# Differential attention in a hybrid decoder block: the causal mask added by TensorE, and the two softmax maps combined with one scaling

## The chip, the cores and the metric

The kernel runs on one core of a Trainium2 chip. The metric is the device time of one execution in microseconds (us), the median over several runs. The engines are named as in the profile: PE is TensorE's matmul stream and PEld its weight loads, DVE is VectorE, ACT is ScalarE, POOL is GpSimd, and SP is SyncE, which here only issues DMA transfers.

## What is computed

One decoder layer for 512 tokens of width 1024: an input projection feeds two groups of heads side by side (differential attention and an RWKV-7 mixer), then come an output projection, an expert layer (PEER) that takes most of the time, a gated per-layer embedding and a last norm. The change lies in the differential attention, which has 4 heads, two score maps for each head, and an RMS norm over the 128 output columns of each head:

```python
def diff_attention(z_da, positions, lam_q1, lam_k1, lam_q2, lam_k2, subln_g, lam_init):
    ...
    lam = (jnp.exp(jnp.sum(lam_q1.astype(f32) * lam_k1.astype(f32)))
           - jnp.exp(jnp.sum(lam_q2.astype(f32) * lam_k2.astype(f32))) + lam_init)
    key_pos = jnp.arange(S)

    def block(bi):
        start = bi * Q_BLOCK
        qb = lax.dynamic_slice_in_dim(q, start, Q_BLOCK, axis=3)
        s = jnp.einsum('bhcqd,bhckd->bhcqk', qb, k).astype(f32)
        causal = key_pos[None, :] <= (start + jnp.arange(Q_BLOCK))[:, None]
        pr = jax.nn.softmax(jnp.where(causal, s, -jnp.inf), axis=-1)
        a = pr[:, :, 0] - lam * pr[:, :, 1]
        return jnp.einsum('bhqk,bhkv->bhqv', a.astype(v.dtype), v)
    ...
    o = rms_norm(o, subln_g) * (1.0 - lam_init)
```

## The kernel before

Tokens are worked on in four blocks of 128 (b = 0 to 3). The attention of one block is `da_block`. For each head h it runs both maps c = 0, 1: a matmul on 64 rows of the array (map 0 on rows 0 to 63, map 1 on rows 64 to 127) writes the scores of the block's queries against the nk = 128 (b + 1) keys seen so far into a PSUM tile `psS` (L753); DVE adds the mask to the last 128 columns of it (L754); DVE takes the row maximum (L756); ACT writes the exponentials to `pexp` and their row sum to `st` (L757). With both maps done, DVE inverts the two sums (L758), multiplies one by minus lambda (L759), scales map 0 (L760) and adds the scaled map 1 (L761). PE turns the result around (`pta`, L765), ACT copies it out (`ah`, L769), and after the fourth head PE multiplies with the values (`po`, L776), ACT squares, and DVE does the norm (L780, the small steps of `rstd`, L783). A float32 matmul is two instructions in the trace, so the 32 score matmuls are 64 rows.

`da_block` is a generator that yields after each head, and `mixers` weaves it with three others: `rw_solve` (a chain of small DVE steps, L582 and L584, that solves triangular systems), `rw` (the RWKV states, all engines) and `ple_proj` (matmuls into `accr`, copied by ACT into `pp` and stored by DMA to `pd`, L800). A scheduler then orders the instructions of every engine by its own estimate of when each is ready; each engine, and SP's queue of DMA issues, works strictly in that order. So an instruction that is taken away or added also moves others.

Three things around the change are spoken of below. First, the tiles `pexp`, `ah`, `sol_u` and `xg` share one ring of 14 buffers, so a `pexp` may have to wait until another tile is read for the last time. Second, for each block `rw_solved` loads `xg`, `tt`, `bhr`, `ykr`, `bk` and `uv` through SP's queue (L601 to L613); PE then makes `pwu` (L620), ACT `wu` (L621), PE `pmt` (L632, which reads `bhr`) and `prp` (L639). Third, the constants are made by POOL in `mixer_consts`, between the squares of the input (L838, L840, L842), whose sum gives the row scales of the first norm (`pss`, L847).

Of the kernel before, what the change touches and what calls it, by code (L numbers as in the profile page):

```python
# [24 lines left out]
NEG = -3.0e38  # L25
EPS = 1e-6
# [27 lines left out]
class Kernel:  # L54
# [188 lines left out]
    def mixer_consts(self, pool):  # L243
        nc, a = self.nc, self.a

        def same_chunk(t, keep_le=None):
# [12 lines left out]
            elif keep_le == 2:  # L259
# [19 lines left out]
        self.causal = pool.tile([128, 128], F32, name="causal")  # L279
        nc.gpsimd.memset(self.causal, 0.0)  # L280
        nc.gpsimd.affine_select(self.causal, self.causal, pattern=[[-1, 128]], base=0, channel_multiplier=1,
                                compare_op=OP.is_ge, fill=NEG)

# [456 lines left out]
    def da_block(self, b, qT, kT, vs, psum, out):  # L740
# [4 lines left out]
        av = []  # L745
        for h in range(4):
            st = sm.tile([128, 4], F32, name="sm")
            pq = self.p4("pexp", [128, 2, 512])
            p = [pq[:, 0], pq[:, 1]]
            for c in range(2):  # L750
                o = slice(64 * c, 64 * c + 64)
                ps = psum.tile([128, 512], F32, name="psS", tag="acc", bufs=4)
                nc.tensor.matmul(ps[:, :nk], qT[o, h, :], kT[h // 2][o, h % 2, :nk], start=True, stop=True)  # L753
                nc.vector.tensor_tensor(ps[:, b * 128:nk], ps[:, b * 128:nk], self.causal, op=OP.add)  # L754
                mx = st[:, c:c + 1]
                nc.vector.tensor_reduce(mx, ps[:, :nk], axis=AX.X, op=OP.max, negate=True)  # L756
                nc.scalar.activation(p[c][:, :nk], ps[:, :nk], AF.Exp, bias=mx, accum_out=st[:, 2 + c:3 + c])  # L757
            nc.vector.reciprocal(st[:, 2:4], st[:, 2:4])  # L758
            nc.vector.tensor_mul(st[:, 3:4], st[:, 3:4], self.nlam)  # L759
            nc.vector.tensor_scalar(p[0][:, :nk], p[0][:, :nk], st[:, 2:3], None, op0=OP.mult)  # L760
            nc.vector.scalar_tensor_tensor(p[0][:, :nk], p[1][:, :nk], st[:, 3:4], p[0][:, :nk], op0=OP.mult,  # L761
                                           op1=OP.add)
# [10 lines left out]
        ss = sm.tile([128, 4], F32, name="oss")  # L773
        for h in range(4):
# [5 lines left out]
        nc.vector.tensor_reduce(ss, sq, axis=AX.X, op=OP.add)  # L780
        r = self.rstd(sm, ss, 128, EPS, cols=4, name="ors")
        for h in range(4):
            nc.vector.scalar_tensor_tensor(out[:, h * 128:h * 128 + 128], po[:, h, :], r[:, h:h + 1], self.subln,  # L783
                                           op0=OP.mult, op1=OP.mult)
# [817 lines left out]
```

## Time and profile before

| what | value |
|---|---|
| runs | 1864.88, 1874.73, 1876.71 us; median 1874.73 us |
| the profiled execution's own time | 1859.81 us |
| its span (first to last instruction) | 1857.4 us |
| mean granted TensorE clock in it | 0.966 of full speed |
| stretch in which `da_block` runs (start of its first psS matmul to start of its last L783) | 289.7 to 452.2 us |

The profile gives for each engine how long it was busy, for each group of instructions (line of the source, engine, operation, tiles) its count, its busy time and the mean of one, and what ended the idle time before it. The timeline has one row for each instruction, or for several like ones in a run: start, duration, engine, line, tiles, count, and in brackets how long the engine had been idle before and what released it. In the timeline the start of the next row on an engine says more than the duration, since matmuls, and DVE instructions that don't depend on each other, overlap at their ends. A view of stretches gives busy times and the granted clock between two points of time.

### The profile page before, as it was taken

How to read it: one execution, taken by the hardware profiler on the slowest of the kernel's cores; microseconds unless marked ns; L12 is line 12 of the kernel's file. 1: busy time of each engine (PE TensorE's matmuls, PEld its weight loads, DVE VectorE, ACT ScalarE, POOL GpSimd, SP SyncE). 2: the span in 40 equal slices, each digit the busy share in tenths (PEclk: the TensorE clock that was granted, in tenths of full speed). 3: DMA queues.
4: the chain of work that ended last, by engine and by line, in shares of the span. 5: the costliest groups of instructions: out<-in, count | busy, mean ns of one | idle time of the engine just before them, and what ended most of it. 6: DMA issues, size and time to landing. Idle time of an engine off the chain costs nothing.

```text
span 1857.4 us, 28657 instructions
## 1 busy us (share of the span) xinstructions
PE 1728.6 (93%) x10434; PEld 1465.3 (79%) x10434; DVE 1448.7 (78%) x3233; ACT 739.5 (40%) x1371; POOL 653.0 (35%) x447
## 2 busy tenths in 40 slices
PE   6887987897998987999999999999999999999998
PEld 5755665666777787998777788889899999989886
DVE  6476587667459999987888787887878787878786
ACT  3424342332335654444443433333333333333354
POOL 6662121110126664001111133334545555555530
PEclk9988997889999998999999999999999999999999
DMA  5533224441442343445665678777989898989891
GB/s 171 154 95 97 81 83 91 100 118 34 150 145 83 109 129 100 140 142 192 208 203 201 195 240 272 237 265 274 310 308 310 308 310 305 311 308 313 303 329 65
DMA packets 149842, 361.62 MB, mean 195 GB/s; under 512 B 43859, under 2 KB 58447, under 8 KB 149573
## 3 DMA queue, kind: packets, MB, share of 16 engines
q1 hardware_dynamic: 109924, 221.89, 37.2%
q0 software_dynamic: 36864, 134.23, 21.3%
q10 hardware_dynamic: 2912, 3.67, 0.7%
q8 instruction: 82, 1.34, 0.3%
q14 instruction: 60, 0.48, 0.1%
HBM read 330.51 MB, written 21.36 MB: 189 GB/s over the span
## 4 chain that ended last, share of the span: by engine, by line
PE 68%; DVE 22%; issue 4%; ACT 3%; DMA 1%; POOL 1%; ACTq 0%; SPq 0%; DVEq 0%; POOLq 0%
PE po L1270 21%; PE phid L1134 8%; PE phid L1136 8%; PE phid L1135 8%; PE pg L1239 2%; DVE wlo L132 2%; ACT whi L128 2%; PE acc L201 2%; DVE ids L1083 2%; PE acc L202 2%; PE acc L200 2%; DVE wlo L134 1%; PE psA L538 1%; DVE rest L977 1%; DVE jj L1227 1%
## 5 line engine op out<-in xcount | busy, mean ns | idle before, releaser
L132 DVE TENSOR_TENSOR wlo<-wraw,whi 128x1024 fp32r<-128x1024 f32 x243 | 297.6, 1225 | 150.5 <-ACT whi L128 150.4
L128 ACT ACTIVATE whi<-wraw 128x1024 fp32r<-128x1024 f32 x276 | 291.4, 1057 | 177.7 <-PE phid L1135 59.0
L1136 PE MATMUL phid<-u2dhi,wlo 128*128 128x384 f32 x1024 | 347.7, 340 | 12.7 <-POOL wlo L132 12.7
L1134 PE MATMUL phid<-u2dhi,whi 128*128 128x384 f32 x1024 | 350.9, 343 | 1.0 <-ACT row L1143 1.0
L1135 PE MATMUL phid<-u2dlo,whi 128*128 128x384 f32 x1024 | 346.9, 339 | 0.0
L1293 POOL DMA_INDIRECT row<-in_peer_u_dram,idx x128 | 190.7, 1490 | 404.5 <-DVE row L1305 222.2
L1293 POOL DMA_INDIRECT row<-in_peer_v_dram,idx x128 | 186.1, 1454 | 276.8 <-DVE h L1309 194.8
L1270 PE MATMUL po<-whi,chi 128*128 128x512 f32 x768 | 243.9, 399 | 1.2 <-ACT row L1143 1.2
L1270 PE MATMUL po<-whi,clo 128*128 128x512 f32 x768 | 243.1, 398 | 1.5
L1270 PE MATMUL po<-wlo,chi 128*128 128x512 f32 x768 | 241.4, 395 | 0.0
L1136 PEld LDWEIGHTS phid<-u2dhi,wlo 128*128 128x128 f32 x1024 | 194.7, 190 | 14.8 <-POOL wlo L132 14.8
L1134 PEld LDWEIGHTS phid<-u2dhi,whi 128*128 128x128 f32 x1024 | 194.8, 190 | 5.8 <-ACT row L1143 1.3
L1135 PEld LDWEIGHTS phid<-u2dlo,whi 128*128 128x128 f32 x1024 | 194.4, 190 | 3.7
L1270 PEld LDWEIGHTS po<-whi,clo 128*128 128x128 f32 x768 | 143.0, 188 | 42.0 <-DVE clo L134 8.7
L1270 PEld LDWEIGHTS po<-wlo,chi 128*128 128x128 f32 x768 | 144.4, 188 | 34.3
L1309 DVE SCALAR_TENSOR_TENSOR h<-row,ids,h 128x1024 f32<-128x1024 f32 x128 | 164.0, 1281 | 1.5
L128 ACT ACTIVATE chi<-gelu 128x384 fp32r<-128x384 f32 x128 | 67.4, 526 | 239.8 <-DVE gelu L1247 121.5
L1270 PEld LDWEIGHTS po<-whi,chi 128*128 128x128 f32 x768 | 141.1, 188 | 25.5 <-ACT row L1143 1.5
L1305 DVE SCALAR_TENSOR_TENSOR row<-row,xn 128x1024 f32<-128x1024 f32 x128 | 153.8, 1220 | 0.0
L1143 ACT ACTIVATE gelu<-phid 128x384 f32<-128x384 f32 x86 | 42.3, 492 | 266.9 <-PE phid L1136 266.9
L200 PE MATMUL acc<-whi,uhi 128*128 128x512 f32 (+1 forms) x224 | 91.1, 416 | 18.8 <-ACT whi L128 11.6
L132 POOL TENSOR_TENSOR wlo<-wraw,whi 128x1024 fp32r<-128x1024 f32 x33 | 78.8, 2400 | 68.9 <-ACT whi L128 68.9
(436 smaller groups left out, 2938.0 us busy)
## 6 DMA issues: line engine op xcount, KB each, us to landing
wraw<-in_peer_uT_dram SPq DMA_DIRECT2D x128, 512.0 KB, 3.9
wraw<-in_peer_v_dram SPq DMA_DIRECT2D x128, 512.0 KB, 6.2
wraw<-in_w_in_dram SPq DMA_DIRECT2D x24, 512.0 KB, 6.1
wraw<-in_peer_w_q_dram SPq DMA_DIRECT2D x16, 512.0 KB, 4.4
ahead<-row SPq DMA_DIRECT2D x42, 192.0 KB, 2.3
gelu<-ahead SPq DMA_DIRECT2D x42, 192.0 KB, 3.8
wraw<-in_w_out_dram SPq DMA_DIRECT2D x8, 512.0 KB
zp<-z ACTq DMA_DIRECT2D x12, 224.0 KB, 2.7
```

Of the source, the lines that this page charges most:

```text
L128: self.last_hi = nc.scalar.activation(hi, src, AF.Copy, **({} if g is None else {"scale": g}))
L132: self.last_lo = eng.tensor_tensor(lo, src, hi.bitcast(F32), op=OP.subtract)
L200: nc.tensor.matmul(o, hi[:, k, s], whi, start=(k == 0), stop=False)
L201: nc.tensor.matmul(o, hi[:, k, s], wlo, start=False, stop=False)
L1134: nc.tensor.matmul(ps, whi[:, s], hi[:, k, :], start=(k == 0), stop=False)
L1135: nc.tensor.matmul(ps, whi[:, s], lo[:, k, :], start=False, stop=False)
L1136: nc.tensor.matmul(ps, wlo[:, s], hi[:, k, :], start=False, stop=(k == KC - 1))
L1143: nc.scalar.activation(g, ps, AF.Gelu)
L1270: nc.tensor.matmul(outs[b, e], lhs[:, s], rhs[:, 512 * e:512 * e + 512], start=(c == 0 and rhs is vhi and lhs is chi), stop=(c == NKEY - 1 ...
L1293: nc.gpsimd.indirect_dma_start(out=row, out_offset=None, in_=a["peer_u" if kind == "U" else "peer_v"], in_offset=bass.IndirectOffsetOnAxis ...
L1305: nc.vector.scalar_tensor_tensor(row, row, 1.0, xn0, op0=OP.mult, op1=OP.mult, accum_out=hid0[:, k:k + 1])
L1309: nc.vector.scalar_tensor_tensor(acc0, row, hid0[:, k:k + 1], acc0, op0=OP.mult, op1=OP.add)
```

## The change

The mask becomes a matmul: after each score matmul PE multiplies an identity with the 128x128 mask and accumulates it onto the last 128 columns of `psS`. Mask and identity are copied by POOL into tiles of the matmul type fp32r, and the masked value is -2^127. DVE no longer adds the mask.

Map 0 is left unscaled. With the sums s0 and s1 of the exponentials, DVE forms f = (s0 / s1) times minus lambda and adds f times map 1 to map 0; the result is s0 times what it was. That factor is taken out at the end: the reciprocals r0 of the four s0 (one instruction for each block) multiply the sum of squares twice ahead of the norm's square root and the norm's factor once behind it. The statistics of a block lie in one tile `st` of 128x4x4 and not in one for each head.

```diff
+MASK = -2.0 ** 127
...
-        self.causal = pool.tile([128, 128], F32, name="causal")
-        nc.gpsimd.memset(self.causal, 0.0)
-        nc.gpsimd.affine_select(self.causal, self.causal, pattern=[[-1, 128]], base=0, channel_multiplier=1,
-                                compare_op=OP.is_ge, fill=NEG)
+        causal = pool.tile([128, 128], F32, name="causal")
+        nc.gpsimd.memset(causal, 0.0)
+        nc.gpsimd.affine_select(causal, causal, pattern=[[-1, 128]], base=0, channel_multiplier=1,
+                                compare_op=OP.is_ge, fill=MASK)
+        self.causal = pool.tile([128, 128], F32R, name="causal_r")
+        nc.gpsimd.tensor_copy(self.causal, causal)
+        self.ident_r = pool.tile([128, 128], F32R, name="ident_r")
+        nc.gpsimd.tensor_copy(self.ident_r, self.ident)
...
+        st = sm.tile([128, 4, 4], F32, name="sm")
         for h in range(4):
-            st = sm.tile([128, 4], F32, name="sm")
...
-                nc.vector.tensor_tensor(ps[:, b * 128:nk], ps[:, b * 128:nk], self.causal, op=OP.add)
-                mx = st[:, c:c + 1]
+                nc.tensor.matmul(ps[:, b * 128:nk], self.ident_r, self.causal, start=False, stop=True,
+                                 skip_group_check=True)
+                mx = st[:, c, h:h + 1]
                 nc.vector.tensor_reduce(mx, ps[:, :nk], axis=AX.X, op=OP.max, negate=True)
-                nc.scalar.activation(p[c][:, :nk], ps[:, :nk], AF.Exp, bias=mx, accum_out=st[:, 2 + c:3 + c])
-            nc.vector.reciprocal(st[:, 2:4], st[:, 2:4])
-            nc.vector.tensor_mul(st[:, 3:4], st[:, 3:4], self.nlam)
-            nc.vector.tensor_scalar(p[0][:, :nk], p[0][:, :nk], st[:, 2:3], None, op0=OP.mult)
-            nc.vector.scalar_tensor_tensor(p[0][:, :nk], p[1][:, :nk], st[:, 3:4], p[0][:, :nk], op0=OP.mult,
-                                           op1=OP.add)
+                nc.scalar.activation(p[c][:, :nk], ps[:, :nk], AF.Exp, bias=mx, accum_out=st[:, 2 + c, h:h + 1])
+
+            f = sm.tile([128, 1], F32, name="smf")
+            nc.vector.reciprocal(f, st[:, 3, h:h + 1])
+            nc.vector.scalar_tensor_tensor(f, f, st[:, 2, h:h + 1], self.nlam, op0=OP.mult, op1=OP.mult)
+            nc.vector.scalar_tensor_tensor(p[0][:, :nk], p[1][:, :nk], f, p[0][:, :nk], op0=OP.mult, op1=OP.add)
...
+        r0 = sm.tile([128, 4], F32, name="osr")
+        nc.vector.reciprocal(r0, st[:, 2, :])
...
+        for _ in range(2):
+            nc.vector.tensor_mul(ss, ss, r0)
         r = self.rstd(sm, ss, 128, EPS, cols=4, name="ors")
+        nc.vector.tensor_mul(r, r, r0)
```

In the changed source the lines stand a little lower: the score matmul is L760 there, the mask matmul L761. The scheduler's order shows at three places what moved. A row is one instruction, or several like ones in a run (x2): its line, its operation, the tile it writes and those it reads, and the shape. Ring numbers behind a name are of no matter here.

PE, block 1, heads 0 and 1. `psS` are the scores, `accr` the matmuls of `ple_proj`, `py` those of the RWKV output. Before:

```order
L753 MATMUL psS<-kT_1064,qT 128x256 x2
L236 MATMUL accr<-whi,phi 128x512
L237 MATMUL accr<-wlo,phi 128x512
L238 MATMUL accr<-whi,plo 128x512
L236 MATMUL accr<-whi,phi 128x512
L237 MATMUL accr<-wlo,phi 128x512
L238 MATMUL accr<-whi,plo 128x512
L699 MATMUL py<-state,rtT 32x64 x12
L753 MATMUL psS<-kT_1064,qT 128x256 x2
L236 MATMUL accr<-whi,phi 128x512
L237 MATMUL accr<-wlo,phi 128x512
L238 MATMUL accr<-whi,plo 128x512
```

Now, from the second head on:

```order
L705 MATMUL py<-state,rtT 32x64 x12
L760 MATMUL psS<-kT_1068,qT 128x256
L761 MATMUL psS<-causal_r,ident_r 128x128
L760 MATMUL psS<-kT_1068,qT 128x256
L773 MATMUL pta<-ident,pexp 128x128 x2
L697 MATMUL py<-wu,arb 128x64 x4
L705 MATMUL py<-state,rtT 32x64 x12
L761 MATMUL psS<-causal_r,ident_r 128x128
L237 MATMUL accr<-whi,phi 128x512
L238 MATMUL accr<-wlo,phi 128x512
L239 MATMUL accr<-whi,plo 128x512
```

The two scores of a head stood next to each other; now a mask matmul on all rows of the array stands between them, and the second mask, with the `accr` behind it, comes after two groups of `py`.

SP's queue, the loads for block 1 of the RWKV part. `tt`, `bhr` and `ykr` are loads, `pd` is the store of a `pp` that ACT has yet to write. Before:

```order
L603 DMA xg<-d_xg_82 128x1024
L601 DMA tt<-td_79 32x8x32 x4
L800 DMA pd_70<-pp 128x512
L605 DMA bhr<-d_bh_86 128x1x512
L606 DMA ykr<-d_yk_98 128x512
L613 DMA bk<-d_bh_86 32x16x64
```

Now:

```order
L609 DMA xg<-d_xg_82 128x1024
L607 DMA tt<-td_79 32x8x32 x4
L611 DMA bhr<-d_bh_86 128x1x512
L813 DMA pd_70<-pp 128x512
L612 DMA ykr<-d_yk_98 128x512
L619 DMA bk<-d_bh_86 32x16x64
```

The load of `bhr`, which waits for no engine but only for its place in the queue, now stands ahead of the store. The other loads keep their places behind it.

POOL, near the start of the program. `xt` are the squares of the input and their sums, the rest are constants. Before:

```order
L280 MEMSET causal 128x128
L275 AFFINE_SELECT chunk_ind<-chunk_ind 128x4
L281 AFFINE_SELECT causal<-causal 128x128
L838 TENSOR_TENSOR xt<-xt 128x1024
L277 AFFINE_SELECT chunk_ind<-chunk_ind 128x4
L840 TENSOR_TENSOR xt<-xt 128x1024
```

Now:

```order
L282 MEMSET causal 128x128
L276 AFFINE_SELECT chunk_ind<-chunk_ind 128x4
L288 CAST ident_r<-ident 128x128
L278 AFFINE_SELECT chunk_ind<-chunk_ind 128x4
L283 AFFINE_SELECT causal<-causal 128x128
L851 TENSOR_TENSOR xt<-xt 128x1024
L286 CAST causal_r<-causal 128x128
L853 TENSOR_TENSOR xt<-xt 128x1024
```

The two copies stand in the middle of the squares, ahead of six more of them.

## The prediction

> **What bounds the kernel now.** First the page's head: the whole span, and how busy the engines are in it.
>
> ```profile
> span 1857.4 us, 28657 instructions
> PE 1728.6 (93%) x10434; PEld 1465.3 (79%) x10434; DVE 1448.7 (78%) x3233; ACT 739.5 (40%) x1371; POOL 653.0 (35%) x447
> ```
>
> PE is the busy engine of the whole, but that is an average over stages; the change lies in the attention stage of about 165 us. So I read next the stretches of that stage (us from:to, length; then for PE, PEld, DVE, ACT and POOL the busy time and in brackets the instructions; then the granted clock, the DMA share and GB/s).
>
> ```profile
> 289.40:324.10 34.70, 21.59 (x139) 15.47 (x137) 29.32 (x83) 7.47 (x22) 5.33 (x4) 0.67 0.38 72
> 324.10:349.00 24.90, 23.10 (x225) 16.80 (x225) 15.93 (x65) 9.17 (x29) 0.96 (x1) 0.84 0.36 101
> 349.00:363.80 14.80, 10.32 (x107) 8.45 (x107) 7.93 (x29) 5.28 (x17) 0.00 (x0) 0.77 0.69 134
> 363.80:390.00 26.20, 23.88 (x271) 16.61 (x270) 21.43 (x70) 9.15 (x22) 8.22 (x6) 1.00 0.49 132
> 390.00:408.00 18.00, 17.47 (x121) 11.65 (x120) 10.58 (x29) 6.12 (x16) 3.27 (x3) 0.62 0.30 75
> 408.00:447.00 39.00, 36.18 (x508) 28.34 (x508) 24.71 (x83) 11.01 (x26) 0.00 (x0) 0.96 0.16 32
> ```
>
> Three different limits stand here. Up to 324 us DVE is full (29.32 of 34.70) and PE waits. From 324 on PE is busy nearly all the time (97% at 390 to 408, 93% at 408 to 447), except at 349 to 363.8, where neither PE nor DVE is (10.32 and 7.93 of 14.80) and something else is late. And the clock is low in four of the six: at 0.62 a matmul takes half again as long. So work taken from DVE is worth something only before 324 and where PE waits for DVE, and work given to PE costs time nearly everywhere behind it. How much DVE work waits for PE and not the other way round, the group of the mask addition tells (count; busy us, mean ns; idle us before it and what ended it):
>
> ```profile
> L754 DVE TENSOR_TENSOR psS<-psS,causal 128x128 f32<-128x128 f32 x32 | 9.3, 295 | 23.7 <-PE psS L753 23.6
> ```
>
> These 32 additions are 9.3 us of DVE, but DVE had stood idle 23.6 us for the scores just ahead of twelve of them. Of what DVE saves there, much only lengthens a wait for PE.
>
> **The change, term by term.** The sum is made against the profiled execution's own time, 1859.81 us (its span of 1857.4 and 2.4 around it). That lies 14.92 below the median of the runs shown, 1874.73; the difference is scatter between executions, and I carry the sum over to the median.
>
> *Two copies on POOL, +0.7.* POOL makes constants and squares without a pause up to the last square, and PE waits for that one:
>
> ```profile
> 16.31 0.29 POOL L281 TENSOR_SCALAR_AFFINE_SELECT causal<-causal 128x128 f32<-128x128 f32 x1
> 16.58 1.89 POOL L838 TENSOR_TENSOR xt<-xt 128x1024 f32<-128x1024 f32 x1
> ...
> 33.78 0.38 PE L847 MATMUL pss<-ones,xt 128*128 128x1 f32 x2 [1.98 <-POOL xt L842]
> ```
>
> PE had been idle 1.98 us for the last sum, so whatever POOL gets in addition, PE gets too, and later stages with it. A select over the same 128x128 takes 0.27 from start to start (16.31 to 16.58), which makes 0.54 for two; POOL slows where DVE reads beside it, so I take 0.7, between 0.5 and 1.6. It cannot be a gain.
>
> *Solve stretch, 289 to 324: -1.0.* The chain here is the solve on DVE; at its end ACT, then PE start at once:
>
> ```profile
> 299.65 0.29 DVE L754 TENSOR_TENSOR psS<-psS,causal 128x128 f32<-128x128 f32 x1
> 299.85 0.32 DVE L582 TENSOR_TENSOR sol_p<-sol_x,sol_u 128x98 f32<-128x98 f32 x1
> ...
> 323.65 0.37 ACT L757 ACTIVATE pexp<-psS,sm 128x128 f32<-128x128 f32 x1 [11.60 <-issue]
> 324.16 0.58 PE L753 MATMUL psS<-kT,qT 64*128 64x128 f32 x1 [6.61 <-ACT pexp L757]
> ```
>
> ACT stood 11.60 us ahead of the exponential of head 2: by the order of the tiles its `pexp` takes the ring place of `sol_u`, whose last reader is the solve's last product, and PE's next scores wait 6.61 us for ACT. An addition among the solve steps costs 0.20 (299.65 to 299.85). Three additions and two scalings go from there, 5 x 0.20 = 1.0 (0.6 to 1.4). The masks of heads 0 to 2 that PE gets are hidden in its waits; if DVE were no longer the limit they would cost what the next term says.
>
> *Masks on PE from 324 on, +4.9.* Of the 32, 26 stand there: two of block 0, 24 of blocks 1 to 3. No row shows an fp32r matmul of 128 columns, so I bound it by matmuls of 128 columns that are there:
>
> ```profile
> 325.63 0.47 PE L765 MATMUL pta<-ident,pexp 128*128 128x128 f32 x1
> 326.04 0.47 PE L656 MATMUL pst<-uv,bk 64*64 64x64 f32 x3
> ...
> 370.76 0.44 PE L765 MATMUL pta<-ident,pexp 128*128 128x128 f32 x2
> 371.13 0.56 PE L656 MATMUL pst<-uv,bk 64*64 64x64 f32 x12
> ...
> 427.71 1.16 PE L776 MATMUL po<-dav,ah 128*128 128x128 f32 x8 [0.74 <-ACT ah L769]
> 428.70 1.95 PE L620 MATMUL pwu<-xg,tt 128*128 128x128 f32 x16
> 434.96 2.08 PE L677 MATMUL plg<-g_up,lg 128*128 128x512 f32 x2
> ```
>
> Among others of its own form, one costs (428.70 - 427.71) / 8 = 0.12. Between matmuls on fewer rows, a single one at the low clock costs 0.41 (325.63 to 326.04); a pair at full clock costs 0.37, so a single one about 0.37 - 0.12 = 0.25. In the order about half of the masks have a full-row matmul behind them, the rest stand between scores or states on 64 or 32 rows. I take 0.19, between 0.12 and 0.25: 26 x 0.19 = 4.9, with ends 3.1 and 10.7. It can't be below nothing, since an instruction is added to a full engine. [...]
>
> *Scores that no longer run side by side, +1.5.* Where both score matmuls of a head stand together, the second is free:
>
> ```profile
> 336.06 0.70 PE L753 MATMUL psS<-kT,qT 64*128 64x256 f32 x4
> 336.69 0.50 PE L236 MATMUL accr<-whi,phi 128*128 128x512 f32 x1
> ...
> 348.40 0.70 PE L753 MATMUL psS<-kT,qT 64*128 64x256 f32 x2 [0.26 <-ACT pp L799]
> ```
>
> Four instructions (both maps) take 0.70, and two (one map) take 0.70 as well; each map has its own half of the array. With a mask between them, which uses all rows and must follow the first, that is gone. From 324 on three heads had it in full: heads 0 and 1 of block 1, and head 0 of block 2. [...]
>
> *Loads of RWKV block 1, -5.3.* Here lies the gap of the third stretch. SP's queue, one row of ACT, and PE:
>
> ```profile
> 340.36 1.88 SPq L601 DMA_DIRECT2D tt<-td  x4
> 348.37 0.34 SPq L800 DMA_DIRECT2D pd<-pp  x1
> 348.75 0.59 SPq L605 DMA_DIRECT2D bhr<-d_bh  x1
> ...
> 351.11 0.60 ACT L621 ACTIVATE wu<-pwu 128x512 f32<-128x512 f32 x1 [0.30 <-PE pwu L620]
> ...
> 349.02 2.05 PE L620 MATMUL pwu<-xg,tt 128*128 128x128 f32 x16
> 355.46 0.45 PE L632 MATMUL pmt<-bhr,wu 32*64 32x64 f32 x8 [4.39 <-DMA bhr<-d_bh]
> 355.84 0.94 PE L753 MATMUL psS<-kT,qT 64*128 64x256 f32 x2
> 356.71 2.84 PE L632 MATMUL pmt<-bhr,wu 32*64 32x64 f32 x56
> 361.45 0.69 PE L765 MATMUL pta<-ident,pexp 128*128 128x128 f32 x2
> ```
>
> SP had issued `tt` at 342.24 and then stood until 348.37 at the store of `pp`, since ACT had not written it; `bhr`, which nothing held, stood behind it and came to PE only at 355.46, 4.39 us too late, though `wu` was there at 351.71. In the new order `bhr` is ahead of the store. So the wait ends with `wu`. The same work in block 3, where no load is late, takes 434.96 - 428.70 = 6.3 from `pwu` to the end of `prp`; block 1 takes 361.45 - 349.02 = 12.4, with one score matmul of 0.87 (355.84 to 356.71) in it. 12.4 - 0.87 - 6.3 = 5.3: 3.7 of it wait, the rest the low clock behind the idle time (0.77 in that stretch). Late next is `wu`, then `uv`, whose loads are still behind the store. Bounds: 2.0 if one of these takes the place of `bhr`, 6 with the low clock of the next matmuls. [...]
>
> *Where PE waits for DVE, -2.0.* There are three such places, the ends of the RWKV output of blocks 0, 1 and 2. The rows of the first:
>
> ```profile
> 345.90 0.30 DVE L754 TENSOR_TENSOR psS<-psS,causal 128x128 f32<-128x128 f32 x1
> 346.11 0.16 DVE L704 TENSOR_SCALAR mean<-mean 128x8 f32<-128x8 f32 x1
> 346.17 0.15 DVE L759 TENSOR_TENSOR sm<-sm,nlam 128x1 f32<-128x1 f32 x1
> 346.24 0.35 DVE L760 TENSOR_SCALAR pexp<-pexp,sm 128x256 f32<-128x256 f32 x1
> 346.51 0.69 DVE L705 TENSOR_TENSOR y<-y,mean 128x512 f32<-128x512 f32 x1
> ```
>
> An addition costs 0.21 (345.90 to 346.11), a scaling 0.27 (346.24 to 346.51), a small product 0.06 (346.11 to 346.17). Out go one addition and one scaling at 345.9, three and one at 381 to 388, two and one at 423 to 427: 6 x 0.21 + 3 x 0.27 = 2.1, less 0.1 for the new products. Bounds 1.0 and 3.0, the scaling being dearer with more columns.
>
> *Tail, +0.3.* The last block's three small products and a reciprocal stand in the DVE work that ends the stage: 0.06 to 0.2 each, so 0.2 to 0.6. The reciprocal and multiplication of each head replace their like, at nothing: same count, same size.
>
> Sum: 0.7 - 1.0 + 4.9 + 1.5 - 5.3 - 2.0 + 0.3 = -0.9 us. The profiled execution would take 1858.9, the median 1873.8. No difference that can be measured: about 1% (18.7 us) is what a measurement here can tell from none. Two large terms, the masks and the moved load, cancel; without the load, which the change was not about, it would be slower by 4.4.
>
> **The rivals.**
>
> *Every mask pays the dear price (slower than before).* Place: PE from 324 to 447. [...] For it speaks the 0.41 row; against it that this row was taken at half clock, and that half of the masks have a full-row neighbour. 26 x 0.41 = 10.7 in place of 4.9: +4.9, 1879.6. It decides from 0.23 each (0.19 + 0.9 / 26); to be slower by over 1% a mask would need 0.19 + 19.6 / 26 = 0.94, over twice the dearest row.
>
> *A half-clock stretch goes as well.* At 390 to 408 the granted clock was 0.62, so about 0.76 of 18 us were at half; PE was full, and at full clock the stretch would be shorter by up to 6.8. The stretch before it has short PE gaps that DVE made, which the change shortens, and masks fill some. I price it at 5: -5.9, 1868.8. Against it: no gap there was long, the work that fell idle is of the same kind as now, and a new slow stretch could as well appear elsewhere.
>
> *The load is hidden anyway.* If `uv` or ACT's copies set when the states can start, the 5.3 shrink to 2.0: +2.4, 1877.1. For it: `uv` keeps its place behind the store; against: PE reached a reader of `uv` only at 371.13, behind the second transposes, some 9 us after 361.45.
>
> *The relief of DVE is worth nothing.* If the three places wait for PE in turn, 2.0 and 1.0 go: +2.1, 1876.8. For it speak the 23.6 us of the mask's group, against it the rows at 345.9, where DVE has no idle time.
>
> **How the numbers follow.** Forecast 0.45, dear masks 0.20, clock 0.15, hidden load 0.10, no relief 0.10. The cases lie between 1868.8 and 1879.6. The runs of before reach from 9.9 below their median to 2.0 above it, so the range takes in that much more below (1868.8 - 9.9 = 1858.9) and above (1881.6; with no relief of DVE beside dear masks, +2.1, 1883.7): 1858 to 1884. Faster by over 1% (below 1856.0) needs the clock rival and a low set of runs, 0.06, a part of the clock's 0.15; slower by over 1% (above 1893.5) needs a mask price that no row shows, 0.04, a part of the dear masks' 0.20; within 1%, 0.90.
>
> **What would show it.** The wait of `pmt` for `bhr` is gone from the waits and PE's clock stays at 1.0 behind it (load). The scores stand as runs of two, never four, and a mask's start-to-start cost is 0.12 to 0.25 (masks). The solve's last product ends about 0.3 earlier in spite of 0.7 from POOL. DVE's busy time falls by the 9.3 of the additions and by the 16 scalings, less the new products, and its wait for scores moves to the maximum. The forecast is wrong if a mask takes 0.4 or more, if the idle time before `pmt` is still there under another name, or if the stage's length differs by more than 5 us.

## The result, and the profile after

| | before | after |
|---|---|---|
| median of the first comparison (8 runs each) | 1872.12 us | 1857.53 us |
| their range | 1863.18 to 1876.71 | 1854.85 to 1863.40 |
| ratio, 95% interval | | 0.9938, 0.9909 to 0.9966 |
| the profiled execution, its mean clock | 1859.81 us, 0.966 | 1863.40 us, 0.962 |

The changed kernel is faster by 0.6%, some 11 us, where 0.9 us was forecast: no difference by the bound of 1%, but clear of the measurement's own interval. The ratio puts the time at 1863.1 on the forecast's base (0.9938 x 1874.73), within the range; the raw median lies 0.5 under its lower end. And the profiled executions stand the wrong way round: the one of before was faster than any of its eight runs in the table, the one after the slowest of its eight. Two profiles alone would have said "slower by 3.6". What must be explained is a difference between two sets of executions, not between two traces.

The head of the page after:

```profile
span 1861.7 us, 28696 instructions
PE 1742.9 (94%) x10466; PEld 1475.0 (79%) x10466; DVE 1442.2 (77%) x3201; ACT 739.9 (40%) x1371; POOL 650.5 (35%) x449
```

The attention stage, cut at the same places of the program in both kernels: from PE's first `pwu` of a block to that of the next, and from the last one to PE's start behind its long wait for `olo`. Columns as before (stretch, length; PE, PEld, DVE, ACT, POOL; clock, DMA share, GB/s). Before:

```profile
296.18:349.02 52.84, 40.67 (x349) 30.20 (x348) 42.06 (x131) 14.05 (x45) 3.84 (x3) 0.72 0.31 70
349.02:390.44 41.42, 34.62 (x380) 25.50 (x380) 29.79 (x100) 14.41 (x38) 8.22 (x6) 0.92 0.55 131
390.44:428.70 38.26, 36.11 (x366) 25.50 (x366) 25.39 (x81) 11.71 (x29) 3.27 (x3) 0.82 0.26 60
428.70:461.42 32.72, 23.88 (x319) 19.27 (x317) 22.68 (x67) 11.04 (x21) 2.34 (x1) 0.90 0.09 18
```

After:

```profile
300.21:357.08 56.87, 47.82 (x361) 35.11 (x361) 41.81 (x121) 14.26 (x45) 3.83 (x3) 0.68 0.30 72
357.08:392.88 35.80, 34.56 (x391) 25.05 (x391) 26.62 (x77) 14.35 (x38) 7.96 (x6) 1.00 0.55 143
392.88:434.42 41.54, 39.62 (x374) 27.34 (x373) 24.66 (x82) 11.70 (x29) 3.22 (x3) 0.75 0.23 55
434.42:464.88 30.46, 21.91 (x319) 18.15 (x317) 22.27 (x67) 11.16 (x21) 2.34 (x1) 0.96 0.09 19
```

Together they take 165.24 and 164.67 us, so the two traces differ by 0.6 in the stage; the 3.6 us that the later one is longer came in before the stage, in code that was not changed, where its clock was lower (0.67 against 1.00 between 155 and 165 us). Within the stage the gains and losses are large: +4.0, -5.6, +3.3, -2.3. The last column but two, the clock, goes with those of blocks 1 and 2: it is 1.00 where it was 0.92, and 0.75 where it was 0.82.

The load's place. PE's rows and two of SP's queue in the trace after:

```profile
350.23 0.59 SPq L611 DMA_DIRECT2D bhr<-d_bh  x1
356.05 0.34 SPq L813 DMA_DIRECT2D pd<-pp  x1
...
357.08 2.00 PE L626 MATMUL pwu<-xg,tt 128*128 128x128 f32 x16
359.01 0.45 PE L638 MATMUL pmt<-bhr,wu 32*64 32x64 f32 x8
...
362.40 1.09 PE L645 MATMUL prp<-arb,wu 128*64 128x128 f32 x16 [0.48 <-ACT mt L640]
363.68 0.44 PE L773 MATMUL pta<-ident,pexp 128*128 128x128 f32 x2 [0.18 <-DVE pexp L770]
```

`bhr` is issued at 350.23, ahead of the store at 356.05, and `pmt` starts without a wait. From `pwu` to the end of `prp` block 1 takes 363.68 - 357.08 = 6.6 us in place of 12.4.

A mask's price, from one start to the next, on PE after:

```profile
343.08 0.70 PE L760 MATMUL psS<-kT,qT 64*128 64x256 f32 x2
343.70 0.33 PE L761 MATMUL psS<-causal_r,ident_r 128*128 128x128 f32 x1
343.96 0.70 PE L760 MATMUL psS<-kT,qT 64*128 64x256 f32 x2
344.58 0.33 PE L761 MATMUL psS<-causal_r,ident_r 128*128 128x128 f32 x1
344.75 0.45 PE L237 MATMUL accr<-whi,phi 128*128 128x512 f32 x1
```

Two score matmuls of a map 0.62, the mask 0.26 ahead of the next scores (343.70 to 343.96) and 0.17 ahead of a full-row matmul (344.58 to 344.75); so a head takes 1.67 where it took 0.63.

The solve, on DVE after:

```profile
319.24 0.29 DVE L764 TENSOR_REDUCE sm<-psS 128x1 f32<-128x128 f32 x1 [1.08 <-PE psS L761]
...
320.37 0.29 DVE L764 TENSOR_REDUCE sm<-psS 128x1 f32<-128x128 f32 x1 [0.58 <-PE psS L761]
```

The additions are gone, but the maximum waits in the chain of the solve for the mask, which stands behind `accr` on PE.

### The profile page after: what moved, and what is told of

It reads as the page before. It is cut to its first block, busy times and chain, and to the rows that moved or that the text cites. A ratio compares the mean times of both kernels' runs of the same rounds, so it can differ in the third digit from the quotient of the medians.

```text
span 1861.7 us, 28696 instructions
## 1 busy us (share of the span) xinstructions
PE 1742.9 (94%) x10466; PEld 1475.0 (79%) x10466; DVE 1442.2 (77%) x3201; ACT 739.9 (40%) x1371; POOL 650.5 (35%) x449
## 4 chain that ended last, share of the span: by engine, by line
PE 68%; DVE 23%; issue 4%; ACT 3%; DMA 1%; POOL 1%; ACTq 0%; SPq 0%; DVEq 0%; POOLq 0%
PE po L1283 21%; PE phid L1147 8%; PE phid L1149 8%; PE phid L1148 8%; PE pg L1252 2%; DVE wlo L133 2%; ACT whi L129 2%; DVE ids L1096 2%; PE acc L202 2%; PE acc L203 1%; PE acc L201 1%; PE psA L544 1%; PE psS L760 1%; DVE rest L990 1%; DVE wlo L135 1%
## 5 line engine op out<-in xcount | busy, mean ns | idle before, releaser
L202 PE MATMUL acc<-wlo,uhi 128*128 128x512 f32 (+1 forms) x224 | 92.9, 415 | 11.3 <-DVE wlo L135 11.2
```

The costliest lines, as they stand in the source:

```text
L202: nc.tensor.matmul(o, hi[:, k, s], wlo, start=False, stop=False)
```

## The experiments

Each ran against the kernel before on the same chip. The clock column is the mean over a kernel's runs of the granted clock; n counts its runs.

| kernel | edit | median us (n) | ratio, 95% interval | clock |
|---|---|---|---|---|
| b_again | before, unaltered | 1869.25 (12) | 0.9981, 0.9957 to 1.0004 | 0.9593 |
| a_again | after, unaltered | 1858.31 (7) | 0.9926, 0.9901 to 0.9951 | 0.9651 |
| mask_only | masks on PE, old scaling | 1860.37 (9) | 0.9946, 0.9921 to 0.9971 | 0.9653 |
| scale_only | unscaled map 0, masks on DVE | 1860.66 (10) | 0.9945, 0.9914 to 0.9976 | 0.9629 |
| b_pd | before, stores of `pp` on ACT's queue | 1872.89 (12) | 1.0021, 0.9998 to 1.0045 | 0.9560 |
| b_fill | before, with 32 matmuls of zeros | 1875.76 (12) | 1.0027, 1.0006 to 1.0048 | 0.9583 |
| s_pd | scale_only, stores on ACT's queue | 1852.65 (6) | 0.9915, 0.9886 to 0.9944 | 0.9650 |
| a_mask2 | after, each mask twice | 1864.76 (9) | 0.9968, 0.9953 to 0.9982 | 0.9650 |
| a_late1 | after, the stage ends 0.73 later | 1858.26 (12) | 0.9953, 0.9927 to 0.9979 | 0.9653 |
| a_late4 | after, the stage ends 2.9 later | 1863.14 (12) | 0.9982, 0.9956 to 1.0008 | 0.9622 |
| a_keep | after, zeros added between `pmt` | 1873.27 (12) | 1.0030, 1.0005 to 1.0054 | 0.9597 |
| a_add | after, 32 additions of zeros on DVE | 1868.60 (12) | 0.9985, 0.9960 to 1.0010 | 0.9626 |

### Both kernels again

> The changed kernel once more, unaltered, for a second profiled execution and for the ratio. The first profiled executions (1859.8 us before, 1863.4 after) are each at the edge of its kernel's runs, and the one after enters the attention stage 4.0 us later for reasons that lie in code that was not changed. Theory A (work: the path got shorter by the terms of the sum): the ratio stays near 0.994, and the profiled execution, near 1857, shows the attention stage (first scores to the wait for the last split) 5 to 11 us shorter than before. Theory B (clock: some executions of before lose a half-clock stretch that the changed kernel does not lose): the executions of before fall again in a group near 1864 and one near 1875, those of the changed kernel do not, and two executions of the same clock differ by no more than 3 us.

> The kernel before, unaltered, timed against itself: a ratio of 1.000 within 0.003. Theory A: a profiled execution of 1870 to 1876 us is longer than that of 1859.8 by waits in the attention stage or in front of it. Theory B: it has the same waits, but a mean granted clock of about 0.955 to 0.96 in place of 0.966, and the rows show one more stretch of some 10 to 20 us at half clock that the execution of 1859.8 did not have.

Every run lists its mean clock, and with that the two kernels come together. Over 109 runs of before (those that the experiments were compared with, and b_again) the clock lies between 0.951 and 0.968 and the time falls by 1.5 us for each 0.001 of it; over the 15 runs of after it lies between 0.962 and 0.967. A straight line fitted through each kernel's runs gives its time at a clock of 0.966: 1858.6 us before (95%: 0.6 either way) and 1857.5 after (0.6). Such lines are meant below where a kernel's line is spoken of. The three runs of before that had just that clock took 1857.3 to 1858.0 us, the six of after 1857.1 to 1858.6. So the work of the two kernels differs by about 1 us, and the other 10 are clock: the means are 0.9589 and 0.9655, and 6.6 x 1.5 = 9.9. Theory B had the cause right and its picture partly: the runs of before don't fall in two groups, they spread. Theory A falls: in a_again's profile the stage takes 164.9 us (296.91 to 461.83), 0.3 less than the 165.2 of before and not 5 to 11.

The profile of b_again (1873.29 us, clock 0.957) shows the executions that before usually has. Two stretches of it that the first profile of before ran at full clock, at least in part:

```profile
402.40:422.80 20.40, 20.40 (x134) 13.25 (x133) 9.00 (x23) 2.96 (x9) 3.28 (x3) 0.50 0.33 82
521.80:532.10 10.30, 9.29 (x28) 6.96 (x29) 4.61 (x7) 2.39 (x4) 0.19 (x1) 0.50 0.32 89
```

The first is in block 2 of the attention (10.3 us at half clock there in the first profile, 20.4 here), the second in the output projection, behind the stage, in code that the change doesn't touch.

How the clock changes is seen when the trace of before is cut where it does:

```profile
356.20:363.00 6.80, 6.71 (x79) 5.31 (x78) 3.59 (x9) 3.18 (x12) 0.00 (x0) 0.50 0.50 85
363.00:390.30 27.30, 24.98 (x277) 17.55 (x277) 21.99 (x73) 9.95 (x25) 8.22 (x6) 1.00 0.49 133
390.30:393.70 3.40, 3.40 (x19) 3.40 (x17) 3.08 (x10) 0.60 (x1) 0.00 (x0) 0.50 0.02 5
393.70:397.10 3.40, 2.87 (x52) 1.78 (x51) 1.39 (x2) 2.56 (x8) 0.00 (x0) 1.00 0.12 19
397.10:407.40 10.30, 10.30 (x48) 5.81 (x48) 5.81 (x15) 2.96 (x9) 3.27 (x3) 0.50 0.43 105
407.40:434.70 27.30, 24.89 (x350) 19.23 (x348) 19.78 (x68) 9.33 (x23) 0.00 (x0) 1.00 0.21 47
434.70:438.10 3.40, 3.40 (x13) 2.11 (x9) 1.54 (x3) 0.00 (x0) 0.00 (x0) 0.50 0.26 41
438.10:458.60 20.50, 15.27 (x213) 12.57 (x212) 13.93 (x46) 7.30 (x11) 2.34 (x1) 1.00 0.01 2
```

The clock is 1.00 or 0.50, and every stretch is a multiple of 3.41 us long (27.30 is eight, 6.80 two, 20.50 six). All changes of an execution, over the whole program, lie on one such raster, but the raster's place against the program differs from execution to execution: in the profiles of the ten kernels down to a_mask2 in the table the stage's end lay anywhere from 0.04 to 2.98 us ahead of a line. So the same work falls into other windows each time, and a single time is a draw.

### Each part alone

```diff
-                nc.vector.tensor_tensor(ps[:, b * 128:nk], ps[:, b * 128:nk], self.causal, op=OP.add)
+                nc.tensor.matmul(ps[:, b * 128:nk], self.ident_r, self.causal, start=False, stop=True,
+                                 skip_group_check=True)
```

is all of mask_only (with the two casts); scale_only is the rest of the change.

> Only the mask as a matmul; map 0 is scaled as before. In the order the load bhr of block 1 stays behind the store pd (one tt as well). Theory A, by the terms of the forecast: +0.7 copies, +4.9 masks, +1.5 scores that no longer run side by side, no gain of the load, -0.6 solve stretch (three additions), -1.3 (six additions): +5.2 us, 1877 by the median of 1872. Theory B: masks fill PE's gaps, the half-clock stretch is not lost, and it takes 1858 to 1862 although the load still comes late.

> Only the unscaled map 0; DVE adds the mask as before. In the order the load bhr stays behind the store pd here too. Theory A: -0.4 solve stretch (two scalings), -0.8 (three scalings), +0.3 tail: -0.9 us, 1871. Theory B: PE's work is the same as before, so its executions fall in the same two groups as those of before, with a median of 1868 to 1874. If each part alone gives a half of the 11.6 us, both theories are wrong in where they put the gain.

What is on record for mask_only on `bhr` is wrong: its trace has the load at 346.19, ahead of the store at 352.04, as in the changed kernel. So by the forecast's terms it should have come out at about -0.1 and not +5.2. Its time, 1860.37, is the one that theory B gave. scale_only's 1860.66 lies below what either theory allowed (1871; 1868 to 1874). Both parts give about 10 us alone, and together no more than 11 to 14. At clock 0.966 their lines give 1860.0 and 1856.9: against the 1858.6 of before the masks cost 1.4 and the scaling gains 1.7, each hardly more than its uncertainty of some 1.5, and neither explains its own 10 us. Those are clock again.

### The load, a filling, and both without masks

```diff
-                    self.nc.sync.dma_start(self.pd[b][:, 512 * e:512 * e + 512], o)
+                    self.nc.scalar.dma_start(self.pd[b][:, 512 * e:512 * e + 512], o)
```

is b_pd, and with it s_pd is made from scale_only. b_fill keeps DVE's addition and puts ahead of it:

```diff
+                nc.tensor.matmul(ps[:, b * 128:nk], self.ident_r, self.zero_r, start=False, stop=True,
+                                 skip_group_check=True)
```

> The kernel before with one edit: the stores of pp are issued from ACT's queue, so that no load of the RWKV part stands behind them on SP's queue. It does the load's part of the change and nothing else. Theory L (load): the late load of bhr is what costs before both its wait and much of its clock: the 4.4 us of idle time before pmt go, the stretch behind it runs at clock 1.0, the mean clock rises from 0.957 to 0.964 or more with a scatter of a few us, and it takes 1858 to 1862 in place of 1872. Theory W (work only): 5 us less, 1867, with a clock that scatters from 0.953 to 0.966 as before. Theory F (fill: the masks on PE are what keeps the clock up): the wait goes, but the later half-clock stretches stay, 1865 to 1868, scatter as before.

> The kernel before with 32 matmuls added where the change has its masks, which accumulate an identity times a tile of zeros; DVE still adds the mask, and the load of bhr stays behind the store. [...] Theory L: the late load stays and with it the clock: 0.957, and the added work costs 0.7 + 4.9 + 1.5, so 1877 to 1880. Theory W: the same 1879.

> Only the unscaled map 0 (DVE adds the mask), and the stores of pp on ACT's queue: the candidate that should beat both kernels, since PE gets no masks and no load is late. Theory L: no late load, little scatter, and at the same clock 5 us less than the unscaled map alone (1857 at 0.966): 1852 to 1854, below the changed kernel. Theory F: without the masks the clock scatters as in the unscaled map alone (0.956 to 0.968), median 1856 to 1860, no better than the changed kernel.

b_pd did remove the wait. Its PE rows:

```profile
352.50 2.05 PE L620 MATMUL pwu<-xg,tt 128*128 128x128 f32 x16
354.48 0.45 PE L632 MATMUL pmt<-bhr,wu 32*64 32x64 f32 x8
...
357.73 1.87 PE L639 MATMUL prp<-arb,wu 128*64 128x128 f32 x16
359.53 0.69 PE L765 MATMUL pta<-ident,pexp 128*128 128x128 f32 x2
```

`pmt` starts right behind `pwu`, and the block goes from `pwu` to the end of `prp` in 359.53 - 352.50 = 7.0 us. And yet it is not faster at all: the clock is the lowest of all kernels. Its profile ran 34.1 us at half clock in block 2:

```profile
385.20:419.30 34.10, 33.31 (x213) 22.19 (x212) 15.98 (x50) 7.16 (x19) 3.28 (x3) 0.50 0.22 51
```

So theory L falls: the late load costs its wait, but it isn't what takes the clock, and what it gave was lost behind it. Theory W's 1867 isn't met either (1872.89). Theory F falls too: with 32 more matmuls of zeros on PE the clock was 0.9583, no higher than the 0.9593 of b_again, and the time 1.0027 of before. s_pd was the fastest kernel: 0.9915 of before, and at clock 0.966 its line gives 1851.8 (1.7 either way), 5.8 under the changed kernel. It has the load early and no mask on PE. This is the time that theory L gave for it, but not the little scatter: three of its six runs took 1847 us at a clock of 0.968 to 0.969 and three 1858 to 1860 at 0.960 to 0.962, and its median lies in the gap between. Its interval for the ratio overlaps with that of the changed kernel (0.9926, 0.9901 to 0.9951, in a_again), so that it is faster rests on the comparison at equal clock, not on the medians.

### A mask twice

```diff
-                nc.tensor.matmul(ps[:, b * 128:nk], self.ident_r, self.causal, start=False, stop=True,
-                                 skip_group_check=True)
+                for _ in range(2):
+                    nc.tensor.matmul(ps[:, b * 128:nk], self.ident_r, self.causal, start=False, stop=True,
+                                     skip_group_check=True)
```

> The changed kernel with every mask matmul done twice, each with half of the masked value (-2^126); the output is the same. It prices a mask in place: 26 of the 32 lie where PE is full. The forecast has 0.12 for one beside its own form: +3 us, 1861, clock as in the changed kernel. If a mask costs 0.26 wherever it stands (as between 64-row scores in the trace after): +7 us, 1865. If PE's time there were hidden after all: within 1 us, 1858.

PE in its trace, the place of the rows above:

```profile
340.58 0.44 PE L762 MATMUL psS<-causal_r,ident_r 128*128 128x128 f32 x2
340.95 0.70 PE L760 MATMUL psS<-kT,qT 64*128 64x256 f32 x2
341.58 0.44 PE L762 MATMUL psS<-causal_r,ident_r 128*128 128x128 f32 x2
341.85 0.45 PE L237 MATMUL accr<-whi,phi 128*128 128x512 f32 x1
```

Two masks take 0.37 (340.58 to 340.95) and 0.27 (341.58 to 341.85) in place of 0.26 and 0.17: the second costs 0.11, as forecast for one beside its own form. That makes 26 x 0.11 = 2.9 us; the line at clock 0.966 gives 5.4 more than the changed kernel. So the median, 1864.76, is that of the dear price (1865) though the rows show the cheap one, and the rest stays unexplained.

### The end of the stage moved

```diff
+        for _ in range(1 if b == NB - 1 else 0):
+            nc.vector.tensor_scalar(yf, yf, 1.0, None, op0=OP.mult)
         nc.vector.tensor_mul(out, yf, g)
```

With 4 in place of 1 it is a_late4.

> The changed kernel with one DVE instruction more in the chain that ends the attention stage (a multiplication of y by one, 0.73 us); every other engine has the same order. Theory P (phase): the granted clock changes only on a fixed raster of 3.41 us, and in the changed kernel the end of the stage (PE's start behind its last wait for olo) stands 0.88 and 0.95 us ahead of a line of the raster in both profiled executions, since the last long half-clock stretch, which ends on a line, ties the program to it. 0.73 later makes 0.15 to 0.22, where three of the ten profiled executions so far lie between 0.04 and 0.27 and all of them lost a further half-clock stretch some 51 us behind that point. So it takes 1858 + 0.7 + 2 to 5 = 1861 to 1864, with a mean clock of 0.962 to 0.964. Rival (plain work): 1858.6 us, clock 0.966.

> The same with four such instructions, 2.9 us. Theory P: the point lies 1.4 us ahead of a line, between the executions at 0.55 and 1.67 that lost nothing there: 1858 + 2.9 = 1861, clock 0.966 as in the changed kernel, and no half-clock stretch 51 us behind the point. So four instructions cost no more than one, or less. Rival (plain work): 2.2 us more than with one instruction.

Theory P failed. It took for granted that block 2 always has its long half-clock stretch, as in the first two profiles after, which ties the rest to the raster. In a_late1's profile that stretch isn't there. The whole of block 2:

```profile
393.14:425.57 32.43, 30.44 (x374) 22.00 (x373) 25.03 (x82) 11.69 (x29) 3.22 (x3) 1.00 0.33 71
```

32.43 us at clock 1.00, with the same order on PE as in the changed kernel, which took 41.54 at 0.75. So the order of one program allows both. What is known to differ up to there is the place of the raster; that it decides is read from the traces, not shown. Behind it a_late1's stage ended 3.05 us ahead of a line and its output projection did lose two windows, where b_again's, at 2.98, lost three. But a_late4's lost three as well, at 1.90, where theory P expected none. Against 1857.8, the median of the 15 runs of after, one instruction cost 0.5 us and four 5.4; by the lines at clock 0.966 neither costs anything that can be told (1857.2 both).

### The small matmuls

```diff
+            for _ in range(2):
+                nc.tensor.matmul(pm, self.ident_r, self.zero_r[:, None, :].to_broadcast([128, 4, 64]), start=False, stop=True,
+                                 skip_group_check=True)
             nc.scalar.activation(mt[:, c, :, :], pm, AF.Copy)
```

> The changed kernel with two full-row matmuls of 256 columns of zeros behind each of the four groups of pmt in every block (32 in all). Theory T (trigger): a raster window that holds 1.7 us or more of pmt (matmuls on 32 rows) is followed by one at half clock, and in block 2 the half clock then lasts some 20 us because scores and small products follow. With the filling the half-clock stretch of 20.5 us in block 2 is gone or below 10 us; its 20.5 us at half cost up to 10 us, the filling costs 24 x 0.2 = 5 us outside of block 0: 1853 to 1858, clock 0.970. Rival: the fall is not due to pmt: the half-clock stretch stays, and it takes 1858 + 5 to 7 = 1863 to 1865.

The added matmuls don't leave `pmt` as it was, so the states of the RWKV part are other numbers in this kernel; the other instructions and their sizes are the same. Block 2 still ran at half clock, from 399.1 to 423.0 us, and the kernel took 15 us more than the changed one, more than either side allowed. So theory T falls as it was put: in this kernel full-row matmuls of zeros beside `pmt` didn't hold the clock up, and in b_fill 32 of them didn't raise its mean. Whether full-row matmuls of other numbers would, no run shows.

### The additions put back

```diff
                                  skip_group_check=True)
+                nc.vector.tensor_tensor(ps[:, b * 128:nk], ps[:, b * 128:nk], self.zero, op=OP.add)
```

> The changed kernel with the 32 DVE additions put back, as additions of zeros: the masks on PE stay, map 0 stays unscaled, DVE gets its 9.3 us back. (In the order the load of bhr falls behind the store pd again; b_pd showed that this alone does not move the clock.) Theory D (DVE): in three pairs that differ in DVE's work alone or nearly so, the kernel with less of it had the higher clock: before 0.959 and the unscaled map 0.963, b_fill 0.958 and the mask alone 0.965, b_pd 0.956 and s_pd 0.965. [...] So the clock falls to 0.957 to 0.962 and the time is 1865 to 1873. Rival (each kernel lands by chance where its lengths fall on the raster): nothing ties the clock to DVE, 0.963 to 0.967 as in most kernels made from the changed one, and 1858 + 2 = 1860, up to 1863 with the load late.

1868.60 us at a mean clock of 0.9626: ten of the changed kernel's eleven us are gone, the larger half by work (its line gives 1863.5 at 0.966, with the load late again), the rest by clock. That is the time theory D gave, and a clock just above its span. So four pairs agree in sign: with less work on DVE the clock is higher by 0.003 to 0.009. Two of them, this one and b_fill with mask_only, also differ in the place of the load; the other two don't. Small differences of this kind need no cause in DVE's work, though: before itself has means between 0.9577 and 0.9597 on the four chips, and a_late4 lies 0.003 under a_late1 for three more instructions at the end of the stage. So of the pairs without a moved load only b_pd with s_pd (0.009) stands well clear.

## How the order acts on the clock in block 2

How less work on DVE could raise PE's clock no run shows directly; what the traces do show is that it moves PE's instructions against each other and, by the scheduler, changes their order. One such place could be followed in the traces: the `pmt` of RWKV block 2. Before, on PE:

```profile
393.88 0.45 PE L632 MATMUL pmt<-bhr,wu 32*64 32x64 f32 x8
394.64 0.71 PE L632 MATMUL pmt<-bhr,wu 32*64 32x64 f32 x24 [0.31 <-ACT wu L621]
395.57 0.68 PE L632 MATMUL pmt<-bhr,wu 32*64 32x64 f32 x16 [0.22 <-ACT mt L634]
396.18 1.18 PE L753 MATMUL psS<-kT,qT 64*128 64x512 f32 x2
397.29 1.11 PE L632 MATMUL pmt<-bhr,wu 32*64 32x64 f32 x16
398.34 0.48 PE L639 MATMUL prp<-arb,wu 128*64 128x128 f32 x2
```

And in s_pd:

```profile
388.15 0.45 PE L635 MATMUL pmt<-bhr,wu 32*64 32x64 f32 x8
388.91 0.71 PE L635 MATMUL pmt<-bhr,wu 32*64 32x64 f32 x24 [0.31 <-ACT wu L624]
389.84 0.97 PE L635 MATMUL pmt<-bhr,wu 32*64 32x64 f32 x32 [0.22 <-ACT mt L637]
391.00 1.09 PE L642 MATMUL prp<-arb,wu 128*64 128x128 f32 x16 [0.19 <-ACT mt L637]
...
392.03 0.69 PE L757 MATMUL psS<-kT,qT 64*128 64x512 f32 x1
```

From the first `pmt` to `prp` it is 398.34 - 393.88 = 4.46 us before, since two score matmuls on 64 rows (1.11) stand among the `pmt` on 32 rows, and 391.00 - 388.15 = 2.85 in s_pd, where the scores stand behind `prp`. Before, PE is busy 2.87 of 3.40 us in the window from 393.70 to 397.10 (its row stands in the cut above), and the next is at half clock all the same, while in the same trace a window with PE busy for only 1.74 us (349.33 to 352.74) was followed by full clock. So it isn't idle time alone that counts. In the 13 profiles of kernels whose `pmt` is that of before I sorted the windows at full clock that hold over 0.8 us of `pmt`, in blocks 1 to 3, by what else they hold. With at least 0.96 us of `pwu`, `prp`, `plg` or `accr` the next window was at full clock 17 of 18 times; with less it was at half, 22 of 22. The four tiles and the bound were chosen with these windows in view, and one such window in block 0 (a_mask2, 1.08 us) was followed by half clock as well; so this describes the windows and doesn't test a rule.

From that an estimate follows: a window is followed by half clock, or falls, if a stretch without those matmuls covers more than 3.41 - 0.95 = 2.46 us of it. The stretch before takes 3.96 us as long as the clock is full (scale_only has the same order there and stayed at full clock), so it escapes only if a line of the raster parts it near its middle, at (2 x 2.46 - 3.96) / 3.41 = 28% of the places; one of 2.85 escapes at (4.92 - 2.85) / 3.41 = 61%. The profiles, the same from which the rule was drawn, fit: of the eight with the scores among `pmt` (before, b_again, b_pd, b_fill, mask_only, scale_only, a_mask2, a_add) seven ran at half clock there, b_pd from before it on; of the five without (after, a_again, a_late1, a_late4, s_pd) two. If nine falls were dealt out to the 13 by chance, about one deal in eight would part them so or further. In block 1, before, idle time of 4.4 us lengthens the same stretch. After a fall in block 2 the clock stayed at half for 3.4 to 20.5 us (23.9 in a_keep, 34.1 in b_pd), while PE worked on scores, `po` and small matmuls.

This is read from traces, not shown by an experiment: no kernel moved the two score matmuls and nothing else. And it can't be all. scale_only has the order of before at this place and still the higher clock; and in a_keep the window from 395.7 to 399.1 holds three pairs of full-row matmuls of zeros:

```profile
396.54 0.50 PE L643 MATMUL pmt<-zero_r,ident_r 128*128 128x256 f32 x2
...
397.58 0.50 PE L643 MATMUL pmt<-zero_r,ident_r 128*128 128x256 f32 x2
...
398.63 0.50 PE L643 MATMUL pmt<-zero_r,ident_r 128*128 128x256 f32 x2
```

Each pair takes some 0.43 us from start to start (396.54 to 396.97), 1.3 in all, and the next window was at half. So the sum of `pwu`, `prp`, `plg` and `accr` sorts the windows, but what the clock counts stays open, and so does the way by which less work on DVE raises it in scale_only.

## Why the prediction was right or wrong

- *The sum, -0.9.* At equal clock -1.1, with 0.8 either way, so right in total. The kernels also price it in three steps at clock 0.966, each to some 2 us: the scaling -1.7 (before to scale_only; forecast -0.9), the stores off SP's queue -5.1 (scale_only to s_pd; forecast for the load -5.3), and the masks for the additions +5.8 (s_pd to after, with the stores back on SP's queue; the rest of the sum, +5.3). So the two large terms that cancel came out in their sizes. But in scale_only's trace `pmt` doesn't wait for `bhr` (it starts at 359.45, right behind `pwu`), so it isn't shown that those 5.1 are the wait that the forecast named; and the single terms inside the steps were off by more, as follows.
- *Two copies, +0.7.* POOL's rows from the clearing of the mask to the second square got 0.5 longer (16.01 to 19.58 before, 15.55 to 19.60 after); POOL happened to start 0.46 earlier, so PE went on at 33.76 in place of 33.78. In a_again the same rows take 4.49 in place of 3.57 and PE went on at 34.21, 0.43 later. So the term is between nothing and 0.4. That POOL slows beside DVE, for which the forecast took 0.7 and not 0.54, is in POOL's rows before: a select of 128x128 took 0.75 us from start to start with DVE at work (9.67 to 10.42) and 0.24 with DVE idle (15.49 to 15.73). Not every row shows it: the square at 16.58 took 1.85 with DVE at work, and the one at 7.31, nearly all of it with DVE idle, 1.84.
- *Solve stretch, -1.0.* Wrong in sign. From `pwu` to the solve's last product it took 27.4 and 28.5 us before, 29.1 in both profiles after. The forecast saw the masks of block 0 "hidden in its waits", but the maximum stands in DVE's chain and waits for them: 1.08 and 0.58 us in the rows above.
- *Masks, +4.9.* 0.16 to 0.17 where a full-row matmul follows, mostly 0.26 to 0.29 where scores or small ones do, and 0.38 to 0.41 there at half clock, which touches the forecast's own mark of 0.4: about 6.7 for the 26. The end taken for a single one (0.25) was nearly right, the mean too low. DVE's wait for the scores moved to the maximum, as forecast (15.5 us of work, 25.0 of waiting for the mask matmul):

```profile
L764 DVE TENSOR_REDUCE sm<-psS 128x1 f32<-128x128 f32 (+3 forms) x32 | 15.5, 487 | 25.1 <-PE psS L761 25.0
```

- *Scores side by side, +1.5.* No run shows the forecast's 1.5. What the rows after show is 0.62 for two of 256 columns and 0.84 for two of 384 (366.78 to 367.62): 2 x 0.62 + 0.84 = 2.1, with the mask's price beside it and not in it.
- *The load, -5.3.* 12.4 to 6.6 us from `pwu` to the end of `prp`, so -5.8 with a mask more in it; 1.00 in place of 0.92 of the clock. Confirmed as a place by b_pd, which got 7.0. But b_pd's time shows that the 5 us don't reach the end of the program unless the clock holds in block 2.
- *Where PE waits for DVE and the tail, -1.7.* No separate row. If the terms above hold as measured, some 5 to 6 us of gain must lie here or elsewhere for the total of -1.1; this was not settled, so that the terms' errors cancelled is in part luck.
- *The clock.* It stood among the rivals, with one stretch of one execution, "a half-clock stretch goes as well", -5.9, and with 0.15. The step that failed is the one that carried the sum to the median: "the difference is scatter between executions". Those 14.92 us between the profiled execution and the median were not neutral. Some 11 of them are clock, (0.966 - 0.9589) at 1.5 us for each 0.001: half-clock windows that most executions of before have and the profiled one had not. The rest is the draw of three runs, whose median lies 3.9 above that of all 109 (1870.85). The change takes away about 10 of those 11, and why it does stays open. That the time on the forecast's base, 1863.1, lies within the range is luck as far as the mechanism goes: the lowest of the forecast's cases was 1868.8, and it is the scatter of the runs of before, added to the ends, that took the range down to it.

## What to carry to other kernels

When the runs of a kernel spread by half a per cent, look at each run's mean clock before reading its profile, and compare two kernels at equal clock as well as by their medians: the first tells what the edit did to the work, and what the medians differ by beyond that is clock. In this kernel a stretch of small matmuls (on 32 or 64 rows) longer than about 2.5 us, by the estimate above, or an idle PE often stood ahead of half clock (in the trace of before PE was busy for 1.52 us or less of the 3.41 ahead of 15 of the 18 falls); the traces suggest to keep other small matmuls out of such a stretch, but no run tried that alone. And an edit that a scheduler sees moves things on engines it wasn't meant for: here the clock that came with the edit was worth more than the instructions that were taken out.

## What the runs showed of the hardware

In all 14 profiles the granted clock of the one core at work is either 1.00 or 0.50 and changes only on a raster of 3.41 us whose place differs between executions (the stage's end lay 0.04 to 2.98 us ahead of a line). In before an `accr` matmul of 512 columns took 0.23 us from start to start at 1.00 (337.50 to 337.73) and 0.42 at 0.50 (462.44 to 462.86). The 22 windows counted above, which were followed by half clock, held 1.5 to 2.4 us of `pmt` (32x64), and PE was busy in 65 to 100% of each (100% in a_mask2 from 356.64 to 360.05). Windows at full clock with over 1.7 us of `pst` (64x64, in sequences of 16 and more) all held it, as with 2.86 us in block 3 of before (441.52 to 444.93), and at half clock each one with 2.5 us or more of `pst` was followed by full clock. What exactly is counted stays open.

In the gap in front of `pmt` before, PE was busy 0.73 of the 3.41 us ahead of the half clock at 356.20 (the 0.77 in the prediction is the mean of the stretch that holds the gap). The falls in block 2 came with less idle time, as the one behind 2.87 of 3.40 us busy.
